# Rotary embedding on one core: the first slab loaded in two DMAs, the last slab through GpSimd's ring

**Chip, cores, metric.** One core of one Trainium2 chip. The time is device microseconds of the whole kernel; most runs of one kernel agree within 0.3%. A run is called slow when it lies over 1.5% above the fastest of its kernel, and fast otherwise; all comparisons below are between fast runs. The span is the time from the first to the last instruction of the one profiled execution.

## The reference

```python
batch, seq, dim, num_heads = 16, 512, 1024, 16      # float32
x1, x2 = x[..., :half_dim], x[..., half_dim:]       # per head: 32 + 32
rotated = concatenate([x1 * cos - x2 * sin,
                       x1 * sin + x2 * cos], axis=-1)
```

33.55 MB are read and 33.55 MB written; there are only three arithmetic operations for each element. A kernel like this is made of transfers.

## The kernel before

The input is cut into eight slabs of 4 MB: 128 partitions with 32 KB each, contiguous in memory. Five slab buffers rotate. SyncE issues the loads, ScalarE the stores: each puts its DMAs on a ring (queue) of its own, from which the 16 DMA engines take the packets, and a DMA has landed when its completion is signalled. For each slab ScalarE casts to bf16, VectorE does two products and a sum, ScalarE casts back into the slab buffer, and the buffer is stored.

```python
def load(s):
    slab[s] = slabs.tile([P, W], f32, tag="slab", name="slab")      # slots = 5 buffers
    return nc.sync.dma_start(out=slab[s], in_=dram(x, s))

load(0)
... # cos and sin tables (64 KB each) loaded from GpSimd's queue: table[0], table[1]
for s in range(1, slots):        # loads 1 to 4 are issued once the cos table is in
    tc.add_manual_dep(load(s).ins, table[0].ins.name, ...)
...
cast(passes[0])                  # ScalarE: xb <- slab, one pass ahead
for i, (s, r, n) in enumerate(passes):
    if i + 1 < len(passes):
        cast(passes[i + 1])
    ...                          # VectorE: two tensor_mul, one tensor_add
    nc.scalar.copy(out=xs, in_=xu)                                  # ScalarE: slab <- xb
    if r + n == rpp:
        nc.scalar.dma_start(out=dram(out_flat, s), in_=slab[s])     # store s
        if s + slots < nslabs:
            load(s + slots)      # loads 5, 6, 7 wait for stores 0, 1, 2
```

A pass is a whole slab, or half of one for slabs 0, 6 and 7.

## Time and profile before

| | before |
|---|---|
| median time | 162.2 us (161.92 to 162.39) |
| span of the profiled run | 160.4 us |
| busy VectorE / ScalarE | 68% / 71% |
| DMA engines | 90% or more in 38 of 40 slices |
| bytes | 67.24 MB, 419 GB/s over the span |

The table is read from the bottom: the bytes over the rate make up nearly the whole span, and no compute engine is near 100%. The lines themselves stand in the prediction. Three more things, all from the packet records of the trace: a 32 KB row is one packet of 1.213 us on one of 16 DMA engines; rings that have work take turns, a packet each; and the DMA engines have a **lag**, which is time t less (bytes moved by t) / (432.2 GB/s), the rate being 16 x 32,768 B / 1.213 us. A flat lag means full rate; each step up is lost time. Before, the lag is 2.6 us from t = 5 on (the start), goes to 3.55 between 39 and 44 us (when the first store joins the loads) and is nearly flat from there (3.30 at 150 us).

### The profile page before, as it was taken

To read this page: it belongs to the slowest core of one execution; us is meant where nothing else is said; L and a number is where in the kernel's file an instruction comes from. 1 tells how busy PE (TensorE), PEld (TensorE's weight loads), DVE (VectorE), ACT (ScalarE), POOL (GpSimd) and SP (SyncE) were. 2 spreads that over 40 slices of the span, in tenths; PEclk is the share of its full clock that TensorE was granted. 3 is DMA by queue.
4 is the path that set the end of the run, shared out by engine and by line. 5 is a ranking of instruction groups with operands and counts; after the bars stand their busy time and mean duration, and the time that the engine had idled before them with its cause. 6 is when DMAs were issued, how large, how long until landed. Compare 5 with 4: busy or idle time off the path is not lost.

```text
span 160.4 us, 169 instructions
## 1 busy us (share of the span) xinstructions
PE 1.0 (1%) x8; PEld 0.8 (1%) x8; DVE 108.5 (68%) x34; ACT 113.5 (71%) x23; POOL 3.4 (2%) x12
## 2 busy tenths in 40 slices
PE   0011000000000000000000000000000000000000
PEld 0010000000000000000000000000000000000000
DVE  0003799999989979997996099939749599930000
ACT  3006939998998999899907997099995999462000
POOL 7000000000000000000000000000000000000000
DMA  7999999999999999999999999999999999999995
GB/s 245 425 409 409 474 425 400 466 441 392 384 400 400 507 400 400 466 441 392 441 474 392 433 482 392 425 482 400 400 507 400 400 474 433 392 449 466 392 433 221
DMA packets 2368, 67.24 MB, mean 419 GB/s; under 512 B 288, under 2 KB 288, under 8 KB 320
## 3 DMA queue, kind: packets, MB, share of 16 engines
q1 hardware_dynamic: 1152, 33.55, 49.5%
q10 hardware_dynamic: 1152, 33.55, 48.4%
q0 software_dynamic: 64, 0.13, 0.2%
HBM read 33.69 MB, written 33.55 MB: 419 GB/s over the span
## 4 chain that ended last, share of the span: by engine, by line
DMA 59%; ACT 17%; issue 9%; DVE 4%; SPq 0%; ACTq 0%; POOLq 0%
DMA slab<-in_x_dram 39%; DMA out_dram<-slab 15%; ACT slab L146 11%; ACT xb L119 6%; DMA raw<-in_cos_dram 4%; DVE xb L140 1%; DVE xb L143 1%; DVE slab L140 1%; SPq L62 0%; ACTq L146 0%; POOLq L167 0%
## 5 line engine op out<-in xcount | busy, mean ns | idle before, releaser
L119 ACT CAST xb<-slab 128x4096 bf16<-128x4096 f32 (+1 forms) x11 | 56.6, 5155 | 27.5 <-DMA slab<-in_x_dram 26.2
L146 ACT CAST slab<-xb 128x4096 f32<-128x4096 bf16 (+1 forms) x11 | 56.6, 5153 | 3.5 <-DVE xb L143 3.5
L140 DVE TENSOR_TENSOR slab<-xb,tab 128x4096 bf16<-128x4096 bf16 (+1 forms) x11 | 35.9, 3260 | 19.9 <-ACT xb L119 19.8
L140 DVE TENSOR_TENSOR xb<-xb,tab 128x4096 bf16<-128x4096 bf16 (+1 forms) x11 | 35.9, 3261 | 0.3
L143 DVE TENSOR_TENSOR xb<-xb,slab 128x4096 bf16<-128x4096 bf16 (+1 forms) x11 | 35.9, 3261 | 0.3
L110 DVE CAST tab<-acc 128x1024 bf16<-128x1024 f32 x1 | 1.2, 1225 | 12.5 <-PE acc L104 12.5
L119 ACT ACT_TABLE_LOAD x1 | 1.3, 1283 | 0.7 <-PEq L167 0.7
L104 PE MATMUL acc<-tab,pick 128*128 128x128 bf16 x8 | 1.0, 305 | 11.5 <-POOL tab L98 11.5
L92 POOL TENSOR_SCALAR_AFFINE_SELECT pick<-pick 128x128 bf16<-128x128 bf16 x4 | 1.0, 288 | 0.1
L104 PEld LDWEIGHTS <-pick 128*128 128x128 bf16 x8 | 0.8, 136 | 11.4 <-issue 8.0
L73 POOL DMA_DIRECT2D raw<-in_cos_dram x1 | 0.7, 674 | 0.8 <-POOLq L167 0.8
L89 POOL MEMSET pick<- 128x512 bf16 x1 | 0.5, 543 | 0.0
L98 POOL CAST tab<-raw 128x256 bf16<-128x256 f32 x1 | 0.4, 396 | 6.9 <-DMA raw<-in_sin_dram 6.9
L73 POOL DMA_DIRECT2D raw<-in_sin_dram x1 | 0.5, 534 | 0.0
L167 POOL MEMSET const-float32-0.0<- 128x1 f32 x1 | 0.1, 99 | 0.2 <-issue 0.2
L167 POOL MEMSET const-bfloat16-1.0<- 128x1 bf16 x1 | 0.1, 102 | 0.0
L167 POOL MEMSET const-uint8-127<- 128x1 uint8 x1 | 0.1, 102 | 0.0
L167 POOL MEMSET const-float32-1.0<- 128x1 f32 x1 | 0.1, 99 | 0.0
## 6 DMA issues: line engine op xcount, KB each, us to landing
slab<-in_x_dram SPq DMA_DIRECT2D x8, 4096.0 KB, 24.5
out_dram<-slab ACTq DMA_DIRECT2D x8, 4096.0 KB, 26.6
raw<-in_cos_dram POOLq DMA_DIRECT2D x1, 64.0 KB, 7.0
raw<-in_sin_dram POOLq DMA_DIRECT2D x1, 64.0 KB, 9.0
```

What stands on the lines that cost most here:

```text
L73: table[i] = nc.gpsimd.dma_start(out=view(raw, i * TR * half, (1, TR * half)), in_=bass.AP(tensor=src.tensor, offset=src.offset, ap=[[TR * ...
L89: nc.gpsimd.memset(pick, 0.0)
L92: nc.gpsimd.affine_select(out=part, in_=part, compare_op=mybir.AluOpType.not_equal, fill=1.0 if g < G else -1.0, base=-(g % G), pattern=[[ ...
L98: nc.gpsimd.tensor_copy(out=tab1, in_=raw)
L104: nc.tensor.matmul(view(acc, (i * rpp + g * TR) * hd + h * half, (hd, TR), (1, half)), view(pick, (i * h * G + g) * P, (1, P)), view(tab1, ...
L110: nc.vector.tensor_copy(out=tab, in_=acc)
L119: nc.scalar.copy(out=view(xb[s], r * dim, (1, n * dim)), in_=view(slab[s], r * dim, (1, n * dim)))
L140: nc.vector.tensor_mul(out=t, in0=xu, in1=view(tab, a + r * hd, (hd, n), (0, nh), (1, hd)))
L143: nc.vector.tensor_add(out=xu, in0=xu, in1=view(t2, half, (hd, n * nh), (-half, 2), (1, half)))
L146: nc.scalar.copy(out=xs, in_=xu)
L167: nc = _bacc.Bacc("TRN2", target_bir_lowering=False, num_devices=1)
```

## The change

The intent is to put small packets at the very start of the first load, so that something else can take a turn early, and to take the last load off the ring on which it stands behind load 6.

```diff
     def load(s):
+        queue = nc.sync if s < nslabs - 1 else nc.gpsimd
         slab[s] = slabs.tile([P, W], f32, tag="slab", name="slab")
-        return nc.sync.dma_start(out=slab[s], in_=dram(x, s))
+        return queue.dma_start(out=slab[s], in_=dram(x, s))

-    load(0)
+    slab[0] = slabs.tile([P, W], f32, tag="slab", name="slab")
+    for a, b in ((0, 256), (256, W)):
+        nc.sync.dma_start(out=view(slab[0], a, (1, b - a)),
+                          in_=dram(x, 0, a, b - a))
```

256 elements are 1 KB of each partition.

## The prediction

> **What bounds the kernel now.** I read the page from the top: busy shares, the row of slices with the DMA share, the queues, and then the timeline of the end. The page of the kernel before says:
>
> ```profile
> span 160.4 us, 169 instructions
> PE 1.0 (1%) x8; PEld 0.8 (1%) x8; DVE 108.5 (68%) x34; ACT 113.5 (71%) x23; POOL 3.4 (2%) x12
> DMA  7999999999999999999999999999999999999995
> DMA packets 2368, 67.24 MB, mean 419 GB/s; under 512 B 288, under 2 KB 288, under 8 KB 320
> q1 hardware_dynamic: 1152, 33.55, 49.5%
> q10 hardware_dynamic: 1152, 33.55, 48.4%
> q0 software_dynamic: 64, 0.13, 0.2%
> ```
>
> No compute engine passes 71%, but the 16 DMA engines are at 90% or more in every slice but the first and last. q1 is SyncE's ring (the loads), q10 ScalarE's (the stores), q0 GpSimd's (now only the two tables). A call of the windows view shows the same by stage (columns: stretch, length, busy PE, PEld, DVE, ACT, POOL, clock, DMA share, GB/s):
>
> ```profile
> 0.00:2.00 2.00, 0.00 (x0) 0.00 (x0) 0.00 (x0) 1.26 (x1) 0.97 (x6) 1.00 0.60 164
> 2.00:37.00 35.00, 1.01 (x8) 0.84 (x8) 21.16 (x9) 21.08 (x6) 2.40 (x7) 1.00 0.99 423
> 37.00:44.00 7.00, 0.00 (x0) 0.00 (x0) 6.73 (x2) 6.55 (x2) 0.00 (x0) 1.00 1.03 389
> 44.00:85.00 41.00, 0.00 (x0) 0.00 (x0) 38.20 (x9) 35.35 (x6) 0.00 (x0) 1.00 0.99 428
> 99.00:124.00 25.00, 0.00 (x0) 0.00 (x0) 18.75 (x8) 17.74 (x6) 0.00 (x0) 1.00 1.02 439
> 124.00:145.00 21.00, 0.00 (x0) 0.00 (x0) 15.35 (x7) 17.54 (x5) 0.00 (x0) 1.00 0.99 426
> 145.00:158.00 13.00, 0.00 (x0) 0.00 (x0) 0.00 (x0) 0.24 (x1) 0.00 (x0) 1.00 1.03 444
> ```
>
> From 2 us to 158 us the rate is flat at 423 to 444 GB/s, with one dent (37 to 44, 389 GB/s) where the first store joins. The single packet records say why it is flat: each 32 KB row is one packet of 1.213 us on one DMA engine, 27.0 GB/s, times 16 = 432 GB/s. So the span is a sum: first packet at 1.74 us; 67.24 MB at 432 GB/s = 155.6 us; some 0.6 us because the 16 first packets take 1.81 us on average and not 1.21; some 0.9 us for the dent; last completion at 159.2, end at 160.4. These give 1.7 + 155.6 + 0.6 + 0.9 + 1.2 = 160.0, for a span of 160.4. The chain of waits (59% DMA, the rest ACT and DVE) is only one thread through this; the ring of stores is never empty once it has begun, and that is what I go by. The end of the timeline shows how much room there is (last lines):
>
> ```profile
> 131.10 0.34 ACTq L148 DMA_DIRECT2D out_dram<-slab  x1
> ...
> 141.64 3.60 ACT L146 CAST slab<-xb 128x4096 f32<-128x4096 bf16 x1 [3.46 <-DVE xb L143]
> 145.28 0.34 ACTq L148 DMA_DIRECT2D out_dram<-slab  x1
> ```
>
> Stores 6 and 7 are issued at 131.1 and 145.3, but in the packet records store 5 occupies the engines to 139.8, store 6 to 149.5, store 7 from 148.85 to 159.2. So the last store waits 3.6 us behind store 6; less some 1.2 us from issue to first packet (0.74 to 1.74-2.5 at the start), the compute chain has about **2.4 us of slack**. Anything that makes slab 7 later by more than that is paid in full; anything that makes it earlier is worth nothing.
>
> **What the skill says.** The Trainium skill, "DMA: Bandwidth & Descriptors", section "Issuing engines are not separate DMA queues", says that DMAs of all issuers run on the same 16 engines and interleave, so a second issuer only saves issue time. The trace agrees: with both hardware rings active the total is still 433 GB/s. The same page, "Queues, rings and completion order", has the engines take turns between rings a packet at a time. The trace agrees: q1 and q10 alternate one 32 KB packet each, and a table load (one 4,096 B packet of 0.159 us per engine, at 5.9 us) and its completion (7.25 us) stand exactly one 1.21 us packet of load 0 apart. Its section "SWDGE vs HWDGE vs iDMA" says a software packet is preferably at most 4,096 B; on the GpSimd ring the trace shows only those 4,096 B packets (eight 512 B rows in one), so how a 32 KB row is cut there is **not shown**. "SBUF — State Buffer", section "SBUF: two separate sides", warns that VectorE can lock GpSimd out of writing descriptors in its two-port modes, and a later section ("Who interferes with whom") says tensor_tensor has none; nothing in this trace shows either, as GpSimd issues both its DMAs before VectorE starts.
>
> **Part 1: slab 0 in two DMAs.** Removed: one load of 128 packets of 32 KB. Added: 128 packets of 1 KB and 128 of 31 KB, one more set of 16 completions, one more issue of 0.33 to 0.47 us on SyncE. Bytes are the same. Per-packet cost: the 4,096 B packet takes 0.159 us, an eighth of a 32 KB packet would be 0.152, so some 0.007 us a packet, an estimate from these two; 8 more packets per engine are 0.06 us and a completion 0.009: **+0.07 us** of DMA time. What could it win? The excess of the first packets, 0.6 us. But that excess is the latency to the first bytes, which a 1 KB packet has too: the small DMA brings 8 KB per engine (0.3 us of data), the second DMA is ready some 0.4 us after the first (the issue time), so the stream closes up at about the same moment. I give it 0 to -0.3 us. The tables could get their turn earlier than 5.9 us, if small packets stand ahead of them in place of large ones. That would release loads 1 to 4 before 8.25 us (they wait for the cos table); but load 0 keeps the ring busy to 12.9 us either way, and the table product is ready at 13.74 us while VectorE waits for ScalarE's cast until 16.97. So worth nothing: **0 us**. The first cast now waits for two DMAs, of which the larger lands last at the old 13.3 us.
>
> **Part 2: load 7 on GpSimd's ring.** The load waits for store 2 (slot reuse) until 99.0 us, as before; this wait moves from SyncE to GpSimd, which has nothing else to do. Descriptor writing costs GpSimd perhaps 0.7 us (a table issue is 0.67 and 0.53), off every path. What moves: before, load 7 stood behind load 6 and ran from 104.07 to 122.4, then landed at 123.96. Now it is a third ring from about 100.5 (if it needs as long as the first table from issue to packet, 4.6 us, from 103.6). At 100.5 most engines are at their last load 6 packet, so load 6 is held up by one turn, 1.2 us, and load 7 taking every second turn with store 3 ends up to 2.4 us sooner, near 121.5. ScalarE: the cast of slab 6 slips 104.6 to 105.8 at most, but it then waited 1.83 us for load 7, and that wait is gone; store 7 would be issued near 144.4 and not 145.28. That is inside the slack and buys nothing, since stores 5 and 6 still fill the engines to 149. **0 us.**
>
> Sum: 162.2 + 0.07 - 0.1 (half-believed start) = **162.2 us**, no change.
>
> **Rivals.** (a) *Large software packets.* If all eight 32 KB rows of an engine go as one turn on GpSimd's ring (as the eight 512 B rows do), load 7 runs unbroken for 8 x 1.213 = 9.7 us. Load 6 then lands about 9.4 us later, near 114; the ScalarE chain loses that less the 1.83 us wait it no longer has, so store 7 is issued near 145.3 + 7.6 = 152.9, and 7.6 - 2.4 = 5.2 us are paid: 167.4 us, +3.2%. For it: the merged 4,096 B packet. Against: that packet is also just the preferred size. Chance 0.1. (b) *Small software packets.* If rows are cut at 4,096 B, load 7 gets one eighth of a store's share per turn while stores are pending (1/9 of the engines). From 99 us the stores 3 to 5 and the rest of load 6 are 31 us of work, which at 8/9 lasts to about 134 us; load 7 has then 3.9 of its 9.7 us and lands near 141; the stores 6 and 7 hang on it (ScalarE is in order, and the cast of slab 7 stands before the last cast of slab 6), so the last store is issued near 162 and ends near 174: 176 us, +8%. Chance 0.06. (c) *VectorE locks out the descriptor writer* for an instruction or two of 4.4 us: load 7 starts as late as 108, lands up to 4 us late, and pays up to 1.6 us: 163.8. Against it: the skill on tensor_tensor. (d) *The start really gains* the 0.6 us of the first packets and the tables no longer interrupt: 161.5.
>
> **Range and chances.** Faster by 2% is out of reach: it would need 159.0, and removing start excess and dent in full (1.5 us) only gives 160.7. The middle case, (c) and (d) are 161.2 to 163.8 and about 84%. (a) and (b) make the upper tail. So 162.2, range 161.2 to 163.8; faster 0.01, same 0.85, slower 0.14.
>
> **What would show it.** Right: DMA share 9 in all slices, load 7's rows on q0 as 128 packets of 32 KB taking turns with q10, load 6 landing within 1.5 us of 104.6, load 7 between 121 and 125, the last store issued before 147.5, first packet near 1.74 us, span within 0.5 us of 160.4. Wrong: zeros or low digits in the DMA row between 124 and 150 (slab 7 late, rival b), a long wait of ScalarE for load 6 (rival a), a GpSimd issue of several us (c), or 432 GB/s reached well before 2.5 us (d).

## The result, and the profile after

| | before | after |
|---|---|---|
| median time | 162.21 us (161.92 to 162.39, 4 runs) | 162.41 us (162.38 to 162.46, 4 runs) |
| ratio | | 1.0014, 95% interval 0.9997 to 1.0032 |
| span of the profiled run | 160.4 us | 160.7 us |

A ratio is the mean time of one kernel's fast runs over that of the other's fast runs of the same rounds, so it is not quite the ratio of the medians quoted. The page of the changed kernel, its span, DMA row and queues:

```profile
span 160.7 us, 174 instructions
DMA  5999999999999999999999999999999999999993
DMA packets 2512, 67.24 MB, mean 418 GB/s; under 512 B 304, under 2 KB 432, under 8 KB 464
q10 hardware_dynamic: 1152, 33.55, 48.4%
q1 hardware_dynamic: 1152, 29.36, 43.4%
q0 software_dynamic: 208, 4.33, 6.3%
```

4.19 MB have moved from q1 to q0, the bytes are the same, and there are 144 packets more: 128 of 1 KB and 16 completions. The DMA row is as full as before; only its first digit (5 against 7) and its last (3 against 5) are lower. The windows view by the same stages (columns as in the prediction) shows the difference there:

```profile
0.00:2.00 2.00, 0.00 (x0) 0.00 (x0) 0.00 (x0) 0.00 (x0) 0.97 (x6) 1.00 0.05 16
2.00:37.00 35.00, 1.01 (x8) 0.84 (x8) 19.46 (x9) 22.01 (x6) 2.42 (x7) 1.00 1.01 425
37.00:44.00 7.00, 0.00 (x0) 0.00 (x0) 6.96 (x2) 6.55 (x2) 0.00 (x0) 1.00 1.02 389
44.00:85.00 41.00, 0.00 (x0) 0.00 (x0) 38.53 (x10) 35.99 (x7) 0.00 (x0) 1.00 1.00 432
99.00:124.00 25.00, 0.00 (x0) 0.00 (x0) 18.74 (x8) 18.02 (x5) 0.56 (x1) 1.00 1.00 434
145.00:158.00 13.00, 0.00 (x0) 0.00 (x0) 0.00 (x0) 0.00 (x0) 0.00 (x0) 1.00 1.02 439
```

Every later stage runs at the rate it had, to some 1%. The drop of the first from 164 to 16 GB/s looks worse than it is, since a packet that starts in a window is counted there: 10 of the 16 first packets of 32 KB started before 2.0 us, all of the first 31 KB after it. The packet records give the true size: the 16 first large packets start at 2.42 us on average and take 1.90 us (1.175 is usual for 31 KB, so 0.72 too long). Before, they started at 1.99 and took 1.81 (0.60 too long). So an engine has 39 KB at 4.32 us, where it had 32 KB at 3.80 us; the 7 KB between are worth 0.27 us, which leaves it **0.26 us behind**. Half of this comes from the small packets, which put the first large one 0.43 us later for 0.30 us of data, and half from the first large packet, which is 0.12 us slower still.

The timeline shows what happened to the waits. Three lines of the kernel before, then the changed one (lines between are left out):

```profile
0.74 1.28 ACT L119 ACT_TABLE_LOAD   x1 [0.74 <-PEq L167]
...
13.33 7.11 ACT L119 CAST xb<-slab 128x4096 bf16<-128x4096 f32 x2 [11.31 <-DMA slab<-in_x_dram]
...
123.96 3.61 ACT L119 CAST xb<-slab 128x4096 bf16<-128x4096 f32 x1 [1.83 <-DMA slab<-in_x_dram]
```

```profile
0.74 0.85 SPq L70 DMA_DIRECT2D slab<-in_x_dram  x2
...
13.73 1.28 ACT L125 ACT_TABLE_LOAD   x1 [13.73 <-DMA slab<-in_x_dram]
15.02 7.11 ACT L125 CAST xb<-slab 128x4096 bf16<-128x4096 f32 x2
...
99.84 0.56 POOL L64 DMA_DIRECT2D slab<-in_x_dram  x1 [88.02 <-DMA out_dram<-slab]
104.15 3.61 ACT L125 CAST xb<-slab 128x4096 bf16<-128x4096 f32 x1 [5.42 <-DMA slab<-in_x_dram]
...
123.51 3.60 ACT L125 CAST xb<-slab 128x4096 bf16<-128x4096 f32 x1 [1.82 <-DMA slab<-in_x_dram]
...
144.83 0.34 ACTq L154 DMA_DIRECT2D out_dram<-slab  x1
```

Three lines show the wait for load 6 (104.15), for load 7 (123.51) and the last store (144.83). Two things stand out. ScalarE's table load, which ran at 0.74 us before, now stands behind the wait for slab 0, so the first cast starts at 15.02 us and not at 13.33. The first store is nevertheless issued only 0.4 us later (37.5 against 37.1), because ScalarE had a wait for slab 1 in between. And load 7, issued on GpSimd at 99.84 us, lands at 123.5, where it landed at 123.96: its first packet comes at 104.33 us, 4.5 us after the issue. So there was hardly a head start to gain.

### The profile page after: what moved, and what is told of

It is laid out like the page before. It is cut to its first block, busy times and chain, and to the rows that moved or that the text cites. A ratio compares the mean times of both kernels' runs of the same rounds, so it can differ in the third digit from the quotient of the medians.

```text
span 160.7 us, 174 instructions
## 1 busy us (share of the span) xinstructions
PE 1.0 (1%) x8; PEld 0.8 (1%) x8; DVE 108.4 (67%) x34; ACT 113.6 (71%) x23; POOL 3.9 (2%) x13
## 4 chain that ended last, share of the span: by engine, by line
DMA 43%; ACT 24%; DVE 20%; issue 3%; ACTq 0%; SPq 0%; POOLq 0%
DMA slab<-in_x_dram 22%; DMA out_dram<-slab 20%; ACT slab L152 13%; ACT xb L125 10%; DVE xb L146 7%; DVE slab L146 7%; DVE xb L149 6%; ACT L125 1%; SPq L70 0%; ACTq L154 0%; POOLq L187 0%; ACTq L152 0%; POOLq L64 0%; ACTq L125 0%
## 5 line engine op out<-in xcount | busy, mean ns | idle before, releaser
L64 POOL DMA_DIRECT2D slab<-in_x_dram x1 | 0.6, 559 | 88.0 <-DMA out_dram<-slab 88.0
```

Source lines behind the costliest of these rows:

```text
L64: return queue.dma_start(out=slab[s], in_=dram(x, s))
```

## The experiments

Theory **Start**: the two DMAs of slab 0 lose 0.26 us in the first 4.3 us, since the first packets of the second one are as slow as if no small packets had gone before. Rival **Ring**: GpSimd's ring costs the time. Rival **Table**: the late table load does. Rival **Noise**. To these come tests of the two claims on which the prediction stood: that the DMA engines bind with some slack before the last store, and how a ring's packets share the engines.

The lag in us at some moments, worked out from each kernel's packet records, the end of the last packet (mean of the 16 engines, and the last of them), and the time from that last end to the end of the span:

```
kernel            t=5   t=36  t=50  t=150   last packet: mean, last   to span end
before            2.59  2.62  3.54  3.30    158.85  159.16              1.22
after             2.84  2.87  3.73  3.50    159.05  159.45              1.24
e11 (after again) 2.87  2.90  3.70  3.47    159.01  159.39              1.25
e1 split only     2.82  2.87  3.61  3.38    158.92  159.36              1.47
e2 ring only      2.62  2.65  3.39  3.16    158.71  158.89              1.29
e4 cut at 8 KB    2.40  2.46  3.63  3.40    158.95  159.42              1.47
e7 cut at 16 KB   2.50  3.23  3.20  3.33    158.88  159.53              1.45
e10 store 0 cut   2.68  2.71  3.05  3.00    158.54  158.86              1.45
e12 load 1 cut    2.60  2.70  3.53  3.30    158.84  159.14              1.46
e6 load 7 late    2.60  2.64  3.46  4.13    159.94  160.03              1.23
```

Each row is one profile, so a few hundredths to two tenths of a microsecond of it are chance.

In the time of the last column no data move, and it differs by 0.23 us. At the end of the program SyncE works through its waits for the DMAs, one after another. In the kernel before and the changed one the wait for the last store comes last. In e1, e4, e7, e10 and e12 four waits that are met already stand behind it, each some 0.06 us (in e2, one). The waits view of SyncE, the changed kernel first, then e1 (total, times, longest):

```profile
SPq L187 <- DMA out_dram<-slab: 36.1, 4, 9.6
SPq L187 <- DMA out_dram<-slab: 55.6, 1, 55.6
```

Nobody meant this change of order. It belongs to the program and so to every run of it: the ratios of these five kernels hold some 0.0014 (0.23 of 162.2 us) that is not the cost of their transfers.

**Each part alone.** e1 keeps the split and puts load 7 back on SyncE; e2 keeps GpSimd's ring and loads slab 0 whole.

```diff
 # e1, against the changed kernel          # e2, against the changed kernel
-queue = nc.sync if s < nslabs - 1 ...     -slab[0] = ...; for a, b in ((0, 256), (256, W)): ...
+queue = nc.sync                           +load(0)
```

> Part 1 alone: slab 0 in two DMAs, load 7 back on SyncE's ring. Start theory (the second DMA of slab 0 pays the first-byte latency again, so the engines fall some 0.26 us behind in the first 4.3 us): span about 160.7, as the changed kernel, 0.2 to 0.3 us over the kernel before, i.e. a ratio near 1.0015. Ring theory (GpSimd's ring costs it): span 160.4 and a ratio of 1.000. Noise theory: no reproducible order between the four kernels of this call.

> Part 2 alone: load 7 on GpSimd's ring, slab 0 in one DMA. Start theory: span 160.4 as before, ratio 1.000 within 0.0007; load 7's first packet comes some 4.5 us after its issue, one 32 KB row a turn, as in the changed kernel. Ring theory: span 160.7, ratio near 1.0015.

Measured: e1 162.58 us, ratio **1.0024** (1.0011 to 1.0037); e2 162.26 us, ratio **1.0003** (0.9991 to 1.0015). None of the cost shows on GpSimd's ring: the lag of e2 stays at or below that of the kernel before from t = 50 on, and load 7's first packet came 4.7 us after its issue, as in the changed kernel. Ring falls. Of e1's 0.4 us, 0.23 is the end of the program; the rest is the size of what the changed kernel loses. With that taken off, e1's interval no longer leaves out 1, so e1 alone doesn't rule out Noise. A second run of the changed kernel in later rounds gave the same again:

> The changed kernel once more, as the base for the other kernels of these rounds and to see whether 0.2 us is reproduced: ratio 1.0010 to 1.0025; loss in the first 5 us 2.82 to 2.90 us of lag against 2.6 before; if the first measurement was noise, a ratio of 1.000 within 0.0005.

162.42 us, ratio 1.0016 (1.0003 to 1.0029). The lag at t = 5 is 2.82 to 2.87 in the three profiles with the 1 KB cut in the table and 2.59 to 2.68 in the five where slab 0 is whole, so the start loss is reproduced every time, and with the interval of e11, which leaves out 1, Noise falls.

**The table load.** A tiny ScalarE copy before everything brings the table load back to the start.

```diff
+warm = singles.tile([P, 2], bf16, tag="warm")      # e3, on top of the changed kernel
+nc.gpsimd.memset(warm, 0.0)
+nc.scalar.copy(out=view(warm, 1, (1, 1)), in_=view(warm, 0, (1, 1)))
```

> The changed kernel with a tiny ScalarE copy ahead of everything, so that ScalarE's table load (1.28 us), which the change moved behind the wait for slab 0, comes early again. Start theory: the table load lies on no path that sets the end; the first cast starts near 13.7 in place of 15.0 us and the first store some 0.4 us earlier, but the span stays at 160.7 and the ratio near 1.0015. Table rival (the late first cast costs the 0.2 us): span back at 160.4, ratio 1.000.

Measured 163.47 us, ratio 1.0081: slower than both theories. The reason is in its timeline:

```profile
26.34 3.60 ACT L156 CAST slab<-xb 128x4096 f32<-128x4096 bf16 x1 [5.64 <-DVE xb L153]
...
29.85 7.01 ACT L129 CAST xb<-slab 128x8192 bf16<-128x8192 f32 x1
```

The cast back of slab 0 now stands ahead of the cast of slab 1: the added copy changed the order that the scheduler gave to ScalarE. ScalarE waits 5.64 us for it, the first store is issued at 40.4 us, and later the loads are slowed a second time (lag from 3.5 to 4.4 us at 75 to 79). This experiment tested something else than it was meant to. It was repeated with the order pinned by a dependency, every engine's list being compared with that of the changed kernel beforehand:

```diff
+nc.scalar.copy(out=warm, in_=nc.const_aps.tensor(0.0, [P, 1], f32))   # e9
 ...
+if i == 0: ahead = cast(passes[2])         # emitted early, to be named in a dependency
+back = nc.scalar.copy(out=xs, in_=xu)
+if i == 0: tc.add_manual_dep(back.ins, ahead.ins.name, ...)
```

> The changed kernel with ScalarE's table load early, this time with the order of all other instructions on all engines kept (in the first try it changed). Start theory: first cast near 13.7 us in place of 15.0, first store issued near 37.1 in place of 37.5, yet span 160.6 to 160.8 and the same ratio as the changed kernel run in the same rounds. Table rival: ratio 1.000, 0.2 to 0.4 us under the changed kernel of the same rounds.

The four fast runs give 162.16 to 162.33 us, ratio 1.0007 (0.9993 to 1.0021), against 1.0016 for the changed kernel of the same rounds. The intervals overlap: it may be worth 0.1 us or nothing. The times are inconclusive. The lag speaks against Table: the changed kernel's 0.25 us are lost by t = 5, before any cast, and from t = 5 to 150 it loses 0.66 us where the kernel before loses 0.71.

**Larger cuts.** If the second DMA's delay is the cause, a first DMA with enough data should cover it.

```diff
-for a, b in ((0, 256), (256, W)):          # load 7 on SyncE in both
+for a, b in ((0, 2048), (2048, W)):        # e4: 8 KB and 24 KB
+for a, b in ((0, 4096), (4096, W)):        # e7: 16 KB and 16 KB
```

> Part 1 alone, but cut at 8 KB of each partition in place of 1 KB (load 7 on SyncE). The first DMA then carries 2.4 us of data per engine, enough to cover the second DMA's latency. Start theory: no second excess in the first packets of the 24 KB rows, engines only the 0.07 us of extra packets behind, span 160.4 to 160.5, ratio 1.000 to 1.0007. If it is the mere number of DMAs or packets that costs: as with 1 KB, span 160.7, ratio near 1.0015.

> Slab 0 in two DMAs of 16 KB of each partition, load 7 on SyncE; the first cast waits for the first half alone. Theory that the DMA engines bind: the first cast starts some 5 us earlier (near 8 us) and the first store some 4 to 5 us earlier, and the time does not move: ratio 0.998 to 1.003. If the chain of compute set the end: 3 to 5 us less, ratio 0.97 to 0.98. The share lost in the first 5 us should be as in the kernel cut at 8 KB or smaller than before (2.45 to 2.6 us of lag).

Measured: e4 162.57 us, ratio **1.0028** (1.0016 to 1.0040); e7 162.81 us, ratio **1.0044** (1.0032 to 1.0057). At the start both did what was expected: lag 2.40 and 2.50 at t = 5, better than the 2.59 of the whole load, and in e4 the first 24 KB packets take the usual 0.913 us, with no delay. Yet both are slower. In the profiles 0.25 of e4's 0.52 us and 0.23 of e7's 0.60 us are the end of the program; the rest is a later last packet. In e4 the lag rises by 1.17 from t = 36 to 50 (before 0.92, e2 0.74), and the last engine ends 0.47 us behind the mean (before 0.31, e2 0.18); in e7 that distance is 0.65. So Start explains the 1 KB cut (0.25 us of lag, for 0.2 to 0.3 us of time in the changed kernel) but is not a general cost of splitting: in the larger cuts the loss is made later. e7 was also meant to test the bound by earlier compute. Its first cast and its first two stores in the timeline:

```profile
8.56 3.60 ACT L125 CAST xb<-slab 128x4096 bf16<-128x4096 f32 x1 [6.54 <-DMA slab<-in_x_dram]
...
29.72 0.37 ACTq L154 DMA_DIRECT2D out_dram<-slab  x1
...
57.12 0.34 ACTq L154 DMA_DIRECT2D out_dram<-slab  x1
```

The first cast is 4.8 us and the first store 7.4 us earlier than before, but ScalarE's order changed as in e3 (both casts back of slab 0 stand before the cast of slab 1), so the second store is 5.6 us later (51.50 before) and the last one no earlier (145.65 against 145.28). When this late second store joins the loads, between 60 and 64 us, 0.25 us more are lost. That an early first slab bought nothing fits a bound by the DMA engines; it doesn't prove it, as the chain of compute as a whole did not get earlier.

**Is it the count of DMAs?** e12 cuts load 1 and leaves load 0 whole.

```diff
+for a, b in ((0, 2048), (2048, W)) if s == 1 else ((0, W),):    # e12, on the kernel before
+    d = nc.sync.dma_start(out=view(slab[s], a, (1, b - a)), in_=dram(x, s, a, b - a))
```

> The kernel before with load 1, not load 0, in two DMAs (8 KB and 24 KB of each partition); load 0 whole, ScalarE's table load stays early. It asks why the cuts at 8 and 16 KB cost 0.28 and 0.44% although they start sooner. If the mere count of DMAs and packets costs (one DMA, 128 packets and 16 completions more): ratio 1.002 to 1.004 again, wherever the cut load stands. If it must be the first load: ratio 1.000 within 0.001, lag in the first 5 us 2.6 as before, mean lag at the end 3.1 to 3.35.

162.38 us, ratio 1.0012 (0.9998 to 1.0026): between the two by the time alone. The trace decides: the transfers end when those of the kernel before do (mean 158.84 against 158.85), and the 0.2 us are the end of the program. Its lag grows by 0.10 from t = 5 to 36 (before 0.03); those 0.07 us are the size that the prediction had for the extra packets and completions, but no longer show at t = 50. It does not show where e4 and e7 lose the rest of theirs.

**The first store.** Every kernel so far, e7 apart, loses 0.7 to 1.2 us between t = 36 and 50, when the first store joins the running loads (e7 loses 0.6 us near 34 us, where its store joins). e10 lets it join with smaller packets.

```diff
-nc.scalar.dma_start(out=dram(out_flat, s), in_=slab[s])                # e10, on before
+for a, b in ((0, 2048), (2048, W)) if s == 0 else ((0, W),):
+    nc.scalar.dma_start(out=dram(out_flat, s, a, b - a), in_=view(slab[s], a, (1, b - a)))
```

> The kernel before with store 0 issued as two DMAs, 8 KB of each partition and then 24 KB. The 0.75 to 1.2 us that every kernel so far loses near 40 us, when the first store joins the running loads, would shrink if it is the time of one large packet: to some 0.3 us, ratio 0.996. If it does not depend on the size of the first store packets: loss again 0.75 to 1.2 us, ratio 0.999 to 1.002.

162.09 us, ratio 1.0004 (0.9988 to 1.0019). In the one profile the step is smaller: the lag rises by 0.34 from t = 36 to 50 and by another 0.15 when the 24 KB rows follow. The last packet ends 0.30 us earlier than before, but e2, with a whole store, ends as early (158.89), and the end of the program takes 0.23 us back. The edit also let the first part go out sooner, at 33.93 us and not 37.11, so that packet size is not the only thing that changed. Not settled, and at best 0.3 us.

**The slack before the last store.** Load 7 of the kernel before is held back by a dependency on VectorE's work for slab 5.

```diff
+tc.add_manual_dep(load(nslabs - 1).ins, late.ins.name, ...)   # late: e5 second product, e6 sum
```

> The kernel before, with load 7 held back until VectorE's second product of slab 5 (ends at 101.2 us, the load was issued at 99.0). Slack theory: load 6 holds the ring until 103 us anyway, load 7 lands at most 1 to 2 us later, the last store is issued at most 147 us, inside the 2.4 us of slack: ratio 1.000 within 0.002. If there is no slack (the last store reaches the engines only just in time): span longer by the same 1 to 2 us, ratio 1.006 to 1.012.

> As the one before, held back until VectorE's sum of slab 5 (ends at 105.6 us). Load 7 should then start near 109 us, some 5 us later than before, land near 129 us, and the last store be issued near 150.6 us. Slack theory: 5 minus 2.4 us are paid, span 162 to 163.5, ratio 1.010 to 1.020. If the slack is larger than 5 us: ratio 1.000. If there is none: span 165.5, ratio 1.03.

e5: load 7 issued at 100.33 us, landed at 123.05, 162.16 us, ratio 0.9995 (0.9980 to 1.0010): nothing lost. But nothing was late either: load 7 landed 0.9 us sooner than in the profile before, and the last store was issued at 144.37 us and not 145.28. So e5 used none of the slack and says nothing about it. e6: issued at 104.86 us, ratio **1.0064** (1.0036 to 1.0092), 163.05 us, 0.88 us over the kernel before. Its timeline:

```profile
127.97 3.60 ACT L119 CAST xb<-slab 128x4096 bf16<-128x4096 f32 x1 [6.64 <-DMA slab<-in_x_dram]
...
149.29 0.34 ACTq L148 DMA_DIRECT2D out_dram<-slab  x1
```

Load 7 is 4.0 us later than before (123.96) and so is the last store (145.28), but only 0.9 us are paid. The slack is 3.1 us by this, or 4.0 if the profile of e5, which ran 0.9 us ahead, is taken for the kernel before. The packet records show the gap: store 6 ends at 149.38, store 7's first packet comes at 150.13, 0.84 us after its issue.

**Small packets on GpSimd's ring.** Rival (b) of the prediction, made on purpose: load 7 in rows of 4 KB.

```diff
-return queue.dma_start(out=slab[s], in_=dram(x, s))           # e8, on e2, for load 7 alone
+for h in (0, 1024):
+    queue.dma_start(out=view(slab[s], h, (2048, 4), (1, 1024)), in_=bass.AP(..., offset + h,
+                    ap=[[W, P], [2048, 4], [1, 1024]]))
```

> Load 7 on GpSimd's ring in rows of 4 KB (two DMAs of every second 4 KB of each partition), slab 0 in one DMA: rival b of the prediction made real. If a ring's share goes by the size of its packets (4 KB against the 32 KB of the stores, one packet a turn): load 7 crawls while stores are pending, lands near 141 us, the DMA engines run dry before the last stores, span near 174, ratio near 1.08. If the share does not go by packet size: load 7 lands near 123.5, ratio 1.000 to 1.003.

Measured **176.08 us**, span 174.2, ratio **1.0857** (1.0835 to 1.0880). In the packet records q0 and q10 alternate: 0.159 us for a 4,096 B packet of the load, 1.213 us for a 32 KB packet of the store, so the load gets 0.159 / 1.372 = 12% of an engine. The DMA row of its page, and the cast that waited for load 7:

```profile
DMA  7899999999999989999899999999999900892695
...
140.78 3.60 ACT L128 CAST xb<-slab 128x4096 bf16<-128x4096 f32 x1 [19.50 <-DMA slab<-in_x_dram]
...
162.10 0.34 ACTq L157 DMA_DIRECT2D out_dram<-slab  x1
```

ScalarE waits 19.5 us, and the row has zeros near 140 to 148 us and a low digit before the last store: the stores ran out while load 7 crawled. The prediction had put the landing near 141, the last store near 162 and the time at 176.

## Why the prediction was right

The predicted time was 162.2 us and "same"; it became 162.41 us and the same. By its steps:

- **The bound.** Right. The DMA rate is full in all stages but the start and the dent, and e6 tests it: of 4.0 us by which the last store was later, 3.1 cost nothing and 0.9 were paid; e8 shows what it costs when the stores do run out. Two more tests fell short: e5 delayed nothing, and e7 made only the first slab earlier.
- **The slack, 2.4 us.** The mechanism was right, the size was off: 3.1 us. One mis-sized term is the 1.2 us from a store's issue to its first packet, taken from the start of the kernel; in e6 it is 0.84. That is 0.36 of the 0.7 us; another 0.3 us is that the prediction took the earliest engine to reach store 7 (148.85 us), where the mean of the 16 is 149.17.
- **Part 1.** The extra packets at +0.07 us have that size in e12's trace up to t = 36, in one profile, and are gone from the lag at 50. The term "0 to -0.3 us" for the start had the wrong sign: it is +0.26. The step that failed is that a 1 KB packet has the excess of the first packets too, and that "the stream closes up at about the same moment": the 1 KB packets took 0.05 us on average and at most 0.19, and the excess came with the first 31 KB packets, which are 0.72 us too long. Nor did the tables get their turn earlier: their first packet comes at 6.47 us and not 5.88. That was worth nothing, as foreseen. The forecast stayed at 162.2 us all the same because each of these terms is below 0.3 us; the bound carried it, not they.
- **The first cast.** The prediction let it start at the old 13.3 us. It missed that ScalarE's table load would move behind the wait; the cast starts at 15.02. On the time this shows little or nothing (e9, inconclusive), and none on the lag.
- **Part 2.** Right that it is worth 0 us (e2). Of its two guesses of load 7's start, 100.5 and 103.6 us, the second was near (104.33), so it landed at 123.5, not 121.5, and load 6 was not held up at all.
- **Rivals.** (a) and (b) turned on how a 32 KB row is cut on GpSimd's ring. The trace shows 128 packets of 32,768 B there, 1.213 us each, in turns with the stores: neither. That (b) would have come as told, had rows been cut, is shown by e8. (c) did not occur: GpSimd's issue took 0.56 us although VectorE was at work. (d) did not occur either.

Still open: why the cuts at 8 and 16 KB, which start better, lose 0.3 to 0.4%. Some 0.14% of it is the end of the program; for the rest their traces point to the join of the first store (e4), to the late second store after ScalarE's changed order (e7) and to engines that end further apart, but no run shows the mechanism. No version here beat the kernel before.

## What to carry to other kernels

If the DMA row is full from end to end, count bytes over the measured rate and look only for what fills a gap at the start, at a join of streams, or before the last store; moving a load to another ring changed nothing here, and starting the first slab's compute sooner bought nothing. When two rings compete, compare packet sizes: they take turns by packet, and a ring of 4 KB rows starves beside one of 32 KB rows. When an experiment adds an instruction, compare each engine's order with the original before its time is believed, and SyncE's waits at the end of the program too: here their order alone was worth 0.23 us, as much as the effect that was sought.

## What the Trainium skill lacked or had wrong

- "DMA: Bandwidth & Descriptors", section "SWDGE vs HWDGE vs iDMA": a software packet is given as preferably at most 4,096 B. Here GpSimd's ring sent 32 KB rows as packets of 32,768 B (128 of them, 1.213 us each, as on the hardware rings), and packed only the 512 B rows of the tables to 4,096 B.
- The same page, "Queues, rings and completion order": it tells of turns by packet, but not what follows for unequal packets: 12% of an engine for 4 KB rows beside 32 KB rows, and 8.6% more time for the kernel (e8).
- The same page, "Latency and other measured facts": it gives first bytes after 0.6 us (hardware) and 1 us (software). With busy engines, issue to first packet was 4.5 to 4.7 us on GpSimd's ring (load 7) and 3.8 us on ScalarE's (store 0, 37.11 to 40.94 us; 3.8 to 5.1 in the other kernels); with idle engines 1.0 us on SyncE's (0.74 to 1.74).
- No page that was read has the loss when stores join running loads: 0.7 to 1.2 us near 40 us in most kernels here, while loads that join running stores (load 7 on a ring of its own at 104 us) cost nothing that the lag shows.
